# Two chained transformer blocks on one core: the modulation products in float32 on four column groups, and three of their parts moved to the input products

## The chip, the core and the metric

The kernel runs on one core of a Trainium2 chip. TensorE multiplies matrices into PSUM banks of 128 partitions by 512 float32 columns. VectorE (DVE), ScalarE (ACT) and GpSimd (POOL) work elementwise, and SyncE (SP) issues nearly all transfers from HBM to SBUF, in one order. The metric is the device time of one execution in microseconds; lower is better.

## What is computed

The reference chains two pairs of layers over 256 tokens of width 1024. In the first pair (call its layers 1 and 2) there is also a stream of 256 context tokens. Six vectors of 1024 numbers for each stream, the modulation, come from a condition vector: `m = silu(cond) @ w_mod + b_mod`, split into shift, scale and gate of the attention half and shift, scale and gate of the FFN half. They enter like this:

```python
sh1, sc1, g1, sh2, sc2, g2 = adaln(c, w_mod[l], b_mod[l])
h = modulate(rms_norm(x, norm1_g[l]), sh1, sc1)          # h * (1 + sc1) + sh1
q, k, v, up, ca, cb = project_inputs(h, w_in[l], ...)
...                                                       # differential attention, pool, conv
x = x + g1 * (mix @ w_out[l])
x = x + g2 * swiglu(modulate(rms_norm(x, norm2_g[l]), sh2, sc2), ...)
```

`w_mod[l]` is 1024 by 6144, so each of the six parts is a product of two rows (one for each stream) with a matrix of 4 MB. The second pair of layers has another attention with a table of relative biases, and a gated FFN.

## The kernel before, in words

**Arithmetic.** A float32 product is made of float32r pieces. `piece` (L192) loads 512 KB of weights into a buffer `raw` (4 buffers), ACT rounds it into the high half of a buffer `hl` (4 buffers, 8 KB a partition), and DVE subtracts to make the low half. Three products (high by high, high by low, low by high) of one pass each then stand for one float32 product. A few products are done in plain float32, which the program issues as one matmul and the engine runs as two passes.

**Order.** The kernel is written as generators that yield after each piece of work. `weave` (L1105) takes a step of a main generator and then as many steps of a side generator as a rate says. The engines' queues follow from that by a scheduler which may move instructions past each other, so the listings below are of the program as built. SP's transfers keep the written order (`dma`, L143): a transfer that waits for its buffer holds up all transfers behind it.

**Stages of layer 1.** First the start (`start`, L720): shift and scale of the attention half (2048 columns of `w_mod`) in four chunks of 2 by 256 columns (`mod`), the norm and transposes of 512 tokens (`turn`), and the input products of the convolution, two k at a time (`products`). Then the input products: queries, keys, pool and values, woven with 31 convolution taps on DVE (`conv_mix`). Then the differential attention (`diff_attention`, L1246): 16 steps (4 tiles of 128 tokens by 4 heads), each with two score products of 64 rows (upper and lower half of the array's rows), a softmax on DVE and ACT, transposes and a product with the values in bank `ob`. Woven into it, at 1.8 steps each, is `side_all`: the parts 2, 3 and 4 of the modulation (gate, and shift and scale of the FFN half) by `ada_rows_parts` (L337), 8 pieces of 2 k for each of 2 halves of 512 columns, and then the first two pieces of the output product. Then the output product and the FFN.

**The modulation's products.** In `ada_rows_parts` and `mod` the stationary operand is the condition: `cs` holds high and low parts of both streams in 4 columns. For each k, one matmul of 4 columns takes the high half of the weights and one of 2 columns the low half; both accumulate into 4 rows of a bank. `rows_to_cols` (L369) turns rows into columns by products with a selector of 4 rows (`selc`), `rows_to_gates` (L392) spreads a row over 128 partitions (`selb`).

**The relative biases.** In layer 2 the FFN's side generator `side3` runs `dil_bias` (L1376): 16 transfers of 128 KB from a table in HBM (`dbias`) to two bias tiles, with a yield after each fourth; behind it `prepare2` issues 16 small transfers of gains.

Of the kernel before, what the change touches and what calls it, by code (L numbers as in the profile page):

```python
# [9 lines left out]
F32 = mybir.dt.float32  # L10
F32R = mybir.dt.float32r
# [31 lines left out]

C_ID, C_SELC, C_COS, C_SIN, C_INVF, C_SELB, NCONST = 0, 128, 130, 258, 386, 402, 402 + 256


# [11 lines left out]
def _constants():  # L58
# [15 lines left out]
    for s in range(2):  # L74
        for r in (s, s + 2):
            k[r, C_SELC + s] = 1.0
            k[r, C_SELB + s * P:C_SELB + (s + 1) * P] = 1.0
# [19 lines left out]
class _Kernel:  # L97
    def __init__(self, ctx, tc, io, out):
        self.tc, self.nc, self.io, self.out = tc, tc.nc, io, out
        self.n = 0  # L100
        self.last = self.mark = None
        self.later, self.due = [], []
        pool = lambda name, bufs, **kw: ctx.enter_context(tc.tile_pool(name=name, bufs=bufs, **kw))
        self.big = pool("big", 12)
        self.wraw = pool("wraw", 4)
        self.whl = pool("whl", 4)
        self.s4 = pool("s4", 3)
        self.s2 = pool("s2", 6)
        self.small = pool("small", 24)
# [145 lines left out]
    def setup(self):  # L255
# [10 lines left out]
        self.invf = km[:, C_INVF:C_INVF + 16]  # L266
        self.selc = km[0:4, C_SELC:C_SELC + 2]
        self.selb = [km[0:4, C_SELB + s * P:C_SELB + (s + 1) * P] for s in range(2)]

# [6 lines left out]
        self.mhalf = self.cst.tile([P, 32], F32, tag="mhalf", name="mhalf")  # L276
        nc.gpsimd.memset(self.mhalf, -0.5)


# [8 lines left out]
        nc.vector.scalar_tensor_tensor(si, th, 1.0, cc, op0=ALU.add, op1=ALU.mult)  # L288
        self.cs = self.cst.tile([P, KD, 4], F32R, tag="cs", name="cs")
        self.csf = self.cst.tile([P, KD, 2], F32, tag="csf", name="csf")  # L290
        v = si.rearrange("p (s k) -> p k s", s=2)
        nc.vector.tensor_copy(self.csf, v)
        nc.vector.tensor_copy(self.cs[:, :, 0:2], v)
        nc.vector.tensor_sub(self.cs[:, :, 2:4], v, self.cs[:, :, 0:2].bitcast(F32))

# [25 lines left out]

    def ada_rows_native(self, l, part):
        banks = [self.bank("acc") for _ in range(2)]
        for k in range(KD):
            raw = self.load(self.wview(self.io["w_mod"][l], k, 1, part * D, (part + 1) * D), 1, D)
            for n in range(2):
                self.mm(banks[n][0:2, :], self.csf[:, k, :], raw[:, n * 512:(n + 1) * 512],
                        start=(k == 0), stop=(k == KD - 1))
            yield
        out = []  # L330
        for n in range(2):
            r = self.S2([2, 512])
            self.nc.vector.tensor_copy(r, banks[n][0:2, :])
            out.append(r)
        self._rows = (out, self.ident[0:2, 0:2])

    def ada_rows_parts(self, l, part):  # L337
        out = []
        for n in range(2):
            c0 = part * D + n * 512  # L340
            b = self.bank("acc")
            for k0 in range(0, KD, 2):
                hi, lo = self.piece(self.wview(self.io["w_mod"][l], k0, 2, c0, c0 + 512), 2, 512)
                for kk in range(2):
                    k = k0 + kk
                    self.mm(b[0:4, :], self.cs[:, k, 0:4], hi[:, kk, :], start=(k == 0), stop=False)
                    self.mm(b[0:2, :], self.cs[:, k, 0:2], lo[:, kk, :], start=False, stop=(k == KD - 1))
                yield
            r = self.S2([4, 512])
            self.nc.vector.tensor_copy(r, b[0:4, :])  # L350
            out.append(r)
        self._rows = (out, self.selc)

# [15 lines left out]
    def rows_to_cols(self, dst, bcol):  # L369

        rows, sel = self._rows
        for n in range(2):
            b = self.bank()
            for j in range(4):
                self.mm(b[:, 2 * j:2 * j + 2], rows[n][:, j * P:(j + 1) * P], sel)
# [16 lines left out]
    def rows_to_gates(self, gates):  # L392

        rows, _ = self._rows
        for n in range(2):
# [324 lines left out]
    def start(self):  # L720
# [17 lines left out]
        def mod(c):  # L738

            nonlocal cols  # L740
            rb, r = self.bank(), self.S2([4, 512])
# [10 lines left out]
            nc.scalar.copy(r[0:4, 0:256], rb[0:4, 0:256])  # L752
            if c >= 1:
                part(256, c * 256)
                nc.scalar.copy(r[0:4, 256:512], rb[0:4, 256:512])
            else:
                xload(0)
                turns = self.columns([(0, rows(io["norm1_g"][0]), 0), (KD, rows(io["b_mod"][0, 0:2 * D]), 0)], "c0_0")
                for half in range(2):
                    raw = self.load(self.wview(wm, 4 * half, 4, c * 256, (c + 1) * 256), 4, 256)  # L760
                    xload(1 + half)
                    raw = raw.rearrange("p (a b) -> p a b", a=4)
                    for kk in range(4):
                        k = 4 * half + kk
                        self.mm(rb[0:2, 256:512], self.csf[:, k, :], raw[:, kk, :], start=(k == 0), stop=(k == KD - 1))
                nc.scalar.copy(r[0:2, 256:512], rb[0:2, 256:512])
                xload(3)
                cols = turns()
                nc.vector.tensor_scalar(cols[:, 2 * KD:], cols[:, 2 * KD:], 1.0, None, op0=ALU.add)
            for j in range(2):  # L770
                k = 2 * c + j
                o = ps[:, 4 * k:4 * k + 4]
                self.mm(o[:, 0:2], r[0:4, j * P:(j + 1) * P], self.selc)
                if c >= 1:
                    self.mm(o[:, 2:4], r[0:4, 256 + j * P:256 + (j + 1) * P], self.selc)
                else:
                    nc.tensor.transpose(o[:, 2:4], r[0:2, 256 + j * P:256 + (j + 1) * P], self.ident[:2, :2])
                nc.vector.scalar_tensor_tensor(
# [171 lines left out]
    def layer1(self, l, S, xin, hT):  # L950
# [59 lines left out]
        if not last:  # L1010
            gates = [self.gate(l, 2, s) for s in streams]

            def side():
                yield from self.ada_rows_parts(l, 2)
                self.rows_to_gates(gates)
                for p, d in ((3, 2), (4, 3)):
                    yield from self.ada_rows_parts(l, p)
                    self.rows_to_cols(S.mod[:, d], S.part(p))
# [4 lines left out]
            def side_all():  # L1023
                yield from side()
                for _ in range(2):
                    next(out)
                    yield
# [76 lines left out]

    def weave(self, main, side, rate):  # L1105

        due = 0.0
        for _ in main:
            due += rate
            while due >= 1.0:  # L1110
                due -= 1.0
                next(side, None)
        for _ in side:
            pass

# [260 lines left out]
    def dil_bias(self, out):  # L1376
        a = self.dr[:, :, :]
        for qt in range(2):
# [410 lines left out]
```

## Time and profile before

| what | value |
|---|---|
| time, median of 3 runs | 1683.26 us (1681.92 to 1684.46) |
| the profiled execution | 1682.13 us, span 1680.3 us |
| TensorE busy | 1639.1 us, 98% of the span |
| DVE, ACT busy | 72%, 49% |
| transfers | 262.75 MB, mean 156 GB/s |

The span is the time between the first and last instruction. TensorE's busy time counts matmuls with modelled ends, so overlapping ones are not counted twice. "PEclk" is the granted TensorE clock: 1.00 is 2.4 GHz and 0.50 is 1.2 GHz. A stage's stretch is read with the windows view, which gives each engine's busy time in it; a single instruction's wait stands in brackets in the timeline.

### The profile page before, as it was taken

What the parts mean: (1) busy time and instruction counts of PE and PEld (TensorE: products, weight loads), DVE (VectorE), ACT (ScalarE), POOL (GpSimd) and SP (SyncE); (2) the same over time, 40 slices, a digit from 0 to 9 for tenths busy, and PEclk for the clock granted to TensorE, in tenths of its full rate; (3) what the DMA queues carried; (4) which work ended last, traced back from release to release, by engine and by line L of the source; (5) the groups of instructions that cost most, each with busy time, mean ns of one, the idle gap of its engine ahead of it and who ended that gap; (6) DMA issues with size and microseconds to landing.
All of it is one profiled execution on the core that took longest, in us unless ns stands there. A gap on an engine that the chain in (4) does not pass through costs nothing.

```text
span 1680.3 us, 24688 instructions
## 1 busy us (share of the span) xinstructions
PE 1639.1 (98%) x9399; PEld 1382.5 (82%) x9399; DVE 1205.3 (72%) x2114; ACT 830.6 (49%) x1377; POOL 41.3 (2%) x98
## 2 busy tenths in 40 slices
PE   8999999999999999999799899999999999999998
PEld 5787467878888888886698899788999988799998
DVE  6797876866585545986566557767887887578786
ACT  6344655423222223646543346765555576565553
POOL 1000000000000000000000001000000010000000
PEclk9999899999999999999899999999999999999999
DMA  8622552655375553432269755523566555245653
GB/s 265 192 86 88 184 179 63 189 170 148 124 235 176 166 175 113 139 113 75 89 219 243 199 183 163 155 88 104 188 188 189 175 149 154 70 138 187 189 180 122
DMA packets 183334, 262.75 MB, mean 156 GB/s; under 512 B 11597, under 2 KB 123184, under 8 KB 183216
## 3 DMA queue, kind: packets, MB, share of 16 engines
q1 hardware_dynamic: 182936, 260.85, 50.1%
q8 instruction: 74, 1.21, 0.3%
q10 hardware_dynamic: 280, 0.33, 0.2%
q14 instruction: 44, 0.36, 0.1%
HBM read 259.84 MB, written 1.31 MB: 155 GB/s over the span
## 4 chain that ended last, share of the span: by engine, by line
PE 80%; DVE 7%; DMA 5%; ACT 4%; issue 3%; POOL 1%; SPq 0%; ACTq 0%; DVEq 0%; POOLq 0%
PE aux L155 36%; PE acc L155 33%; PE ob L155 6%; PE aux L245 3%; DMA raw<-in_w_mod_dram 3%; DVE hl L201 2%; ACT hl L199 1%; DVE s L1208 1%; DMA raw<-in_w_ffn_in_dram 1%; DMA raw<-in_w_ffn_out_dram 1%; DMA a<-dbias 0%; ACT s L469 0%; ACT s L1268 0%; ACT jk L417 0%; DMA a<-in_x_dram 0%
## 5 line engine op out<-in xcount | busy, mean ns | idle before, releaser
L155 PE MATMUL acc<-hl,a 128*128 128x512 f32 (+3 forms) x3072 | 718.3, 386 | 7.4 <-ACT hl L199 2.4
L199 ACT CAST hl<-raw 128x1024 fp32r<-128x1024 f32 (+1 forms) x420 | 433.7, 1038 | 500.7 <-PE acc L155 151.0
L155 PEld LDWEIGHTS acc<-hl,a 128*128 128x128 f32 x3072 | 549.9, 189 | 116.6 <-issue 5.2
L201 DVE TENSOR_TENSOR hl<-raw,hl 128x1024 fp32r<-128x1024 f32 (+1 forms) x420 | 503.4, 1203 | 155.9 <-ACT hl L199 153.9
L155 PE MATMUL aux<-a,hl 128*128 128x256 f32 (+1 forms) x4032 | 578.6, 304 | 4.7 <-ACT hl L199 1.6
L155 PEld LDWEIGHTS aux<-a,hl 128*128 128x128 f32 x4032 | 540.2, 192 | 37.4 <-ACT a L470 2.0
L363 DVE SCALAR_TENSOR_TENSOR s<-raw,csf,s 128x1024 f32<-128x1024 f32 x70 | 88.7, 1281 | 43.2 <-DMA raw<-in_w_mod_dram 43.1
L245 PE MATMUL aux<-km,s 128*128 128x128 f32 (+1 forms) x416 | 66.2, 282 | 11.0 <-DVE s L451 8.0
L245 PEld LDWEIGHTS aux<-km,s 128*128 128x128 f32 (+1 forms) x416 | 48.9, 144 | 33.6 <-issue 14.9
L1208 DVE SCALAR_TENSOR_TENSOR s<-up,c,s 128x512 f32<-128x512 f32 (+1 forms) x120 | 70.8, 609 | 0.6
L155 PE MATMUL ob<-a,hl 128*128 128x512 f32 (+1 forms) x288 | 64.3, 372 | 0.0
L155 PEld LDWEIGHTS ob<-a,s 128*128 128x128 f32 x416 | 52.2, 194 | 11.2 <-ACT s L1282 5.4
L155 PEld LDWEIGHTS ob<-a,hl 128*128 128x128 f32 x288 | 51.2, 188 | 9.3
L155 PE MATMUL ob<-a,s 128*128 128x64 f32 (+1 forms) x416 | 56.2, 279 | 0.7 <-ACT s L1665 0.5
L155 PE MATMUL aux<-a,a 96*128 96x256 f32 (+2 forms) x160 | 52.5, 507 | 1.4 <-ACT s L1268 1.3
L532 ACT ACTIVATE s<-aux 128x512 f32<-128x512 f32 x33 | 19.7, 597 | 62.5 <-PE aux L155 62.5
L560 ACT ACTIVATE s<-s,c2a,c2b 128x256 f32<-128x256 f32 x88 | 48.0, 592 | 3.3 <-DVE s L557 3.3
L535 ACT CAST a<-s 128x512 fp32r<-128x512 f32 x33 | 20.4, 618 | 52.9 <-DVE s L534 52.8
L557 DVE TENSOR_TENSOR s<-aux,km 128x512 f32<-128x512 f32 x44 | 30.4, 691 | 20.9 <-PE aux L155 20.9
L533 DVE SCALAR_TENSOR_TENSOR s<-s,aux 128x512 f32<-128x512 f32 x33 | 22.6, 684 | 25.0 <-ACT s L532 25.0
L417 ACT ACTIVATE jk<-a 128x512 bf16<-128x512 f32 x44 | 28.2, 641 | 24.0 <-DVE a L1005 15.3
L1268 ACT ACTIVATE s<-aux,sm,rq 128x512 f32<-128x512 f32 (+1 forms) x48 | 33.8, 705 | 10.7 <-DVE sm L1267 10.4
(244 smaller groups left out, 1306.6 us busy)
## 6 DMA issues: line engine op xcount, KB each, us to landing
raw<-in_w_mod_dram SPq DMA_DIRECT2D x96, 512.0 KB
raw<-in_w_ffn_in_dram SPq DMA_DIRECT2D x88, 512.0 KB
raw<-in_w_up_dram SPq DMA_DIRECT2D x88, 512.0 KB
raw<-in_w_in_dram SPq DMA_DIRECT2D x60, 512.0 KB
raw<-in_w_ffn_out_dram SPq DMA_DIRECT2D x44, 512.0 KB
raw<-in_w_down_dram SPq DMA_DIRECT2D x44, 512.0 KB
raw<-in_w_out_dram SPq DMA_DIRECT2D x32, 512.0 KB
gate<-in_b_mod_dram SPq DMA_DIRECT2D x6, 512.0 KB
```

Of the source, the lines that this page charges most:

```text
L155: self.nc.tensor.matmul(o, lhsT, rhs, start=start, stop=stop)
L199: nc.scalar.copy(hl[:, 0, :n], raw[:, :n])
L201: nc.vector.tensor_sub(hl[:, 1, :n], raw[:, :n], hl[:, 0, :n].bitcast(F32))
L245: self.nc.tensor.transpose(b[:rows, j * P:(j + 1) * P], s, self.ident)
L363: self.nc.vector.scalar_tensor_tensor(accs[s], raw, c, accs[s], op0=ALU.mult, op1=ALU.add)
L417: self.nc.scalar.activation(junk, x[:, h * 512:(h + 1) * 512], AF.Square, scale=D ** -0.5, accum_out=ss[:, h:h + 1])
L533: nc.vector.scalar_tensor_tensor(th, th, 1.0, g, op0=ALU.add, op1=ALU.mult)
L535: nc.scalar.copy(hi, th)
L557: nc.vector.tensor_mul(y, x.rearrange("p (j t) -> p j t", j=2), R2)
L560: nc.scalar.activation(o[:, j, :], y[:, j, :], AF.Identity, scale=wc(1, ff), bias=bc(ff))
L1208: nc.vector.scalar_tensor_tensor(o, up[:, ct, :, k:k + SEQ], w, o, op0=ALU.mult, op1=ALU.add)
L1268: nc.scalar.activation(p[:, c, :], sb[:, :nk * P], AF.Exp, scale=r, bias=nm[:, c:c + 1], accum_out=d[:, c:c + 1])
```

## The change

In float32, without splitting: the condition is stored in `csf`, padded with zeros from 2 to 32 columns for each k. Four k's products go to the four groups of 32 partitions of one bank (`ada_products`), each as one float32 matmul, and the two products for k and k + 4 accumulate in a group. The sum over the four groups is left to the selectors, which now have ones at every 32nd row and 128 rows. The weights come unsplit: in `mod` from `raw`, in the moved parts by transfers of 1 MB into a buffer of the pool `hl`.

The parts 2, 3 and 4 move from the attention's side to a second side of the input products, at rate 1.3; the bank is `ob`. In the attention only the two pieces of the output product stay at its side. `dil_bias` yields after each second transfer. The pool of small tiles shrinks from 24 to 16 buffers.

```diff
-                for half in range(2):
-                    hi, lo = self.piece(self.wview(wm, 4 * half, 4, c0, c0 + 256), 4, 256)
-                    for kk in range(4):
-                        k = 4 * half + kk
-                        self.mm(rb[0:4, o:o + 256], self.cs[:, k, 0:4], hi[:, kk, :], start=(k == 0), stop=False)
-                        self.mm(rb[0:2, o:o + 256], self.cs[:, k, 0:2], lo[:, kk, :], start=False, stop=(k == KD - 1))
+                for half in range(2):
+                    raw = self.load(self.wview(wm, 4 * half, 4, c0, c0 + 256), 4, 256)
+                    self.ada_products(rb[:, o:o + 256], 4 * half, raw.rearrange("p (a b) -> p a b", a=4))
...
+    def ada_products(self, o, k0, raw):
+        for j in range(4):
+            k = k0 + j
+            self.mm(o[j * GROUP:(j + 1) * GROUP, :], self.csf[:, k, :], raw[:, j, :], start=(k < 4), stop=(k >= 4))
+
+    def ada_rows(self, l, part):
         out = []
         for n in range(2):
             c0 = part * D + n * 512
-            b = self.bank("acc")
-            for k0 in range(0, KD, 2):
-                hi, lo = self.piece(self.wview(self.io["w_mod"][l], k0, 2, c0, c0 + 512), 2, 512)
...
+            b = self.bank("ob")
+            for k0 in range(0, KD, 4):
+                raw = self.whl.tile([P, 2, 1024], F32, tag="hl", name=self.nm("wm_"))
+                raw = raw.rearrange("p a (b c) -> p (a b) c", c=512)
+                self.dma(raw, self.wview(self.io["w_mod"][l], k0, 4, c0, c0 + 512))
+                self.ada_products(b, k0, raw)
+                yield
...
-        self.weave(main(), self.conv_mix(S, TQ, len(streams), mB), TAPS[l])
+        self.weave(main(), self.conv_mix(S, TQ, len(streams), mB), TAPS[l], () if last else mods(), 1.3)
...
-            self.weave(self.diff_attention(S, qT, kT, v, rq, q_toks, mA, LAG), side_all(), 1.8)
+            self.weave(
+                self.diff_attention(S, qT, kT, v, rq, q_toks, mA, LAG), (next(out) for _ in range(2)), 0.25)
...
-                if q % (4 * COPIES) == 3 * COPIES:
+                if q // COPIES % 2:
                     yield
```

How the order moves is seen at three places. On TensorE, between the first two pieces of the queries (`hl` is a split piece of `w_in`, `acc` the four banks of the projection, `a` the normalised input), before:

```order
L155 MATMUL acc_735<-hl_738,a_12_149 128x512 x2
L155 MATMUL acc_735<-hl_738,a_14_151 128x512
L155 MATMUL acc_732<-hl_772,a_12_149 128x512 x2
L155 MATMUL acc_732<-hl_772,a_14_151 128x512
L155 MATMUL acc_733<-hl_772,a_12_149 128x512 x2
L155 MATMUL acc_733<-hl_772,a_14_151 128x512
```

and in the changed kernel (`wm` is a piece of `w_mod` as it was loaded):

```order
L156 MATMUL acc_639<-hl_642,a_12_147 128x512 x2
L156 MATMUL acc_639<-hl_642,a_14_149 128x512
L156 MATMUL ob_674<-wm_675,csf 32x512 x4
L156 MATMUL acc_636<-hl_683,a_12_147 128x512
L156 MATMUL acc_637<-hl_683,a_12_147 128x512
```

A group of four products, one on each column group, has come between two pieces of the projection; there are 12 such groups in this stage. On TensorE at the beginning of the attention (`aux<-a,a` is a score product, `cs` the condition), before:

```order
L155 MATMUL aux_1518<-a_114_728,a_113_727 128x512
L155 MATMUL aux_1523<-a_114_728,a_113_727 128x512
L155 MATMUL acc_1531<-hl_1534,cs 4x512
L155 MATMUL acc_1531<-hl_1534,cs 2x512
L155 MATMUL aux_1545<-a_114_728,a_113_727 128x512
L155 MATMUL acc_1531<-hl_1560,cs 4x512
L155 MATMUL acc_1531<-hl_1560,cs 2x512
```

and in the changed kernel (`hl_1637` is a piece of `w_out`):

```order
L156 MATMUL aux_1544<-a_100_628,a_99_627 128x512
L156 MATMUL aux_1549<-a_100_628,a_99_627 128x512
L156 MATMUL aux_1561<-a_100_628,a_99_627 128x512
L156 MATMUL acc_1631<-hl_1637,a_96_622 128x512 x2
L156 MATMUL acc_1631<-hl_1637,a_97_623 128x512
L156 MATMUL acc_1632<-hl_1637,a_96_622 128x512
L156 MATMUL aux_1566<-a_100_628,a_99_627 128x512
L156 MATMUL aux_1578<-a_100_628,a_99_627 128x512
```

The 96 products with `cs` are gone from between the scores, and products of the first pieces of `w_out` stand there earlier. Of the 16 pairs of score products, 10 stood side by side before; now 7 do. On SP in layer 2's FFN (`dbias` the bias table, `raw` weights of the FFN), before:

```order
L147 DMA a_1258_7707<-dbias 16x8x256 x4
L147 DMA raw_7718<-in_w_ffn_out_dram 128x2x512
L147 DMA raw_7735<-in_w_ffn_out_dram 128x2x512
L147 DMA a_1258_7707<-dbias 16x8x256 x4
L147 DMA raw_7759<-in_w_ffn_in_dram 128x4x256
L147 DMA raw_7788<-in_w_ffn_in_dram 128x4x256
```

and in the changed kernel:

```order
L148 DMA a_1208_7463<-dbias 16x8x256 x2
L148 DMA raw_7472<-in_w_ffn_out_dram 128x2x512
L148 DMA raw_7489<-in_w_ffn_out_dram 128x2x512
L148 DMA a_1208_7463<-dbias 16x8x256 x2
L148 DMA raw_7511<-in_w_ffn_in_dram 128x4x256
L148 DMA raw_7540<-in_w_ffn_in_dram 128x4x256
```

Two bias transfers instead of four go between two weight transfers, so that 16 weight transfers are spread among them where 8 were.

## Rows read from the trace of the kernel before

**Rows 1.** The page, part 1: busy time, share and instructions of each engine.

```profile
PE 1639.1 (98%) x9399; PEld 1382.5 (82%) x9399; DVE 1205.3 (72%) x2114; ACT 830.6 (49%) x1377; POOL 41.3 (2%) x98
```

**Rows 2.** Windows by stage: us; PE, PEld, DVE, ACT, POOL; clock, DMA share, GB/s.

```profile
0.00:35.00 35.00, 26.83 (x160) 17.78 (x160) 21.51 (x44) 21.61 (x39) 4.79 (x21) 0.90 0.80 265
35.00:68.00 33.00, 31.79 (x162) 23.66 (x162) 23.20 (x55) 14.34 (x21) 0.20 (x1) 1.00 0.70 222
68.00:162.70 94.70, 94.33 (x482) 79.15 (x481) 83.53 (x145) 40.46 (x64) 2.62 (x5) 1.00 0.34 105
162.70:260.40 97.70, 94.10 (x431) 52.27 (x430) 78.78 (x177) 63.25 (x120) 3.60 (x6) 0.95 0.50 167
191.75:202.00 10.25, 10.25 (x25) 4.61 (x24) 6.59 (x12) 3.19 (x4) 0.00 (x0) 0.50 0.19 55
762.20:803.20 41.00, 40.16 (x192) 25.24 (x192) 29.09 (x76) 24.53 (x51) 2.66 (x6) 1.00 0.25 77
```

**Rows 3.** Windows, instructions on `cs` alone (PE, PEld, DVE), in the attention.

```profile
162.70:260.40 97.70, 27.12 (x96) 7.50 (x96) 0.00 (x0) 0.95 0.50 167
```

**Rows 4.** Timeline of TensorE in the attention: start, us, instruction, [idle before].

```profile
163.73 1.13 PE L155 MATMUL aux<-a,a 64*128 64x512 f32 x4
164.79 1.08 PE L155 MATMUL acc<-hl,cs 128*4 128x512 f32 x4
165.80 1.12 PE L155 MATMUL aux<-a,a 64*128 64x512 f32 x2
166.85 1.33 PE L155 MATMUL acc<-hl,cs 128*4 128x512 f32 x5
...
172.30 2.01 PE L155 MATMUL acc<-hl,cs 128*2 128x512 f32 x8
174.28 1.12 PE L155 MATMUL aux<-a,a 64*128 64x512 f32 x2
176.49 1.09 PE L155 MATMUL acc<-hl,cs 128*4 128x512 f32 x4 [1.09 <-ACT hl L199]
```

**Rows 5.** Groups by shape, attention (162.7 to 260.4 us): busy us, mean ns.

```profile
L155 PE MATMUL aux<-s,km 4*128 4x512 f32 x8 | 5.8, 855 | 0.0
L155 PE MATMUL aux<-km,s 4*128 4x2 f32 x32 | 4.2, 249 | 0.0
...
L201 DVE TENSOR_TENSOR hl<-raw,hl 128x1024 fp32r<-128x1024 f32 x27 | 32.3, 1213 | 0.6 <-ACT hl L199 0.5
```

**Rows 6.** Groups by shape, the half-clock stretch, 191.75 to 202.00 us.

```profile
L155 PE MATMUL aux<-s,km 4*128 4x512 f32 x4 | 3.8, 1096 | 0.0
L155 PE MATMUL aux<-a,a 64*128 64x512 f32 x4 | 2.1, 1138 | 0.0
```

**Rows 7.** Groups by shape, whole span: plain float32 products of 128 rows.

```profile
L155 PE MATMUL aux<-s,ones 128*128 128x512 f32 x16 | 7.5, 592 | 0.0
...
L155 PE MATMUL aux<-raw,csf 128*2 128x256 f32 x16 | 3.8, 379 | 0.0
```

**Rows 8.** Timeline of TensorE in the start.

```profile
47.59 2.00 PE L155 MATMUL aux<-hl,cs 128*4 128x256 f32 x16
```

**Rows 9.** Windows of layer 2's FFN around the bias transfers.

```profile
920.00:935.00 15.00, 12.03 (x76) 10.30 (x74) 7.78 (x9) 5.30 (x6) 0.00 (x0) 1.00 1.12 220
935.00:950.00 15.00, 12.10 (x59) 10.63 (x60) 7.93 (x23) 4.60 (x5) 0.00 (x0) 0.77 0.53 157
935.86:939.27 3.41, 3.41 (x18) 3.41 (x18) 0.30 (x1) 0.00 (x0) 0.00 (x0) 0.50 0.13 42
946.10:949.50 3.40, 3.40 (x9) 2.65 (x9) 3.40 (x19) 2.09 (x2) 0.00 (x0) 0.50 0.89 281
```

**Rows 10.** The chain of waits, 895 to 965 us: start, us, what.

```profile
912.84 13.54 DMA raw<-in_w_ffn_in_dram
...
928.80 9.65 DMA raw<-in_w_ffn_out_dram
```

More of the change, by code (lines that the diff above doesn't have):

```diff
@@ L44 @@
 C_ID, C_SELC, C_COS, C_SIN, C_INVF, C_SELB, NCONST = 0, 128, 130, 258, 386, 402, 402 + 256
+GROUP = 32
 def _bucket(rel):
@@ L74, in _constants @@
     for s in range(2):
-        for r in (s, s + 2):
+        for r in range(s, P, GROUP):
             k[r, C_SELC + s] = 1.0
@@ L108, in __init__ @@
         self.s2 = pool("s2", 6)
-        self.small = pool("small", 24)
+        self.small = pool("small", 16)
         self.cst = pool("cst", 1)
@@ L266, in setup @@
         self.invf = km[:, C_INVF:C_INVF + 16]
-        self.selc = km[0:4, C_SELC:C_SELC + 2]
-        self.selb = [km[0:4, C_SELB + s * P:C_SELB + (s + 1) * P] for s in range(2)]
+        self.selc = km[:, C_SELC:C_SELC + 2]
+        self.selb = [km[:, C_SELB + s * P:C_SELB + (s + 1) * P] for s in range(2)]
         self.R = km[:, C_SELB:C_SELB + SEQ]
@@ L320, in ada_bias @@
         self.dma(dst, self.io["b_mod"][l:l + 1, part * D:(part + 1) * D].partition_broadcast(P))
[L322 to L337, printed above, removed]
+    def ada_products(self, o, k0, raw):
[3 more added lines that the diff above has]
+    def ada_rows(self, l, part):
         out = []
@@ L340, in ada_rows_parts @@
             c0 = part * D + n * 512
-            b = self.bank("acc")
-            for k0 in range(0, KD, 2):
-                hi, lo = self.piece(self.wview(self.io["w_mod"][l], k0, 2, c0, c0 + 512), 2, 512)
[L344 to L347, printed above, removed]
+            b = self.bank("ob")
[4 more added lines that the diff above has]
+                self.ada_products(b, k0, raw)
                 yield
-            r = self.S2([4, 512])
-            self.nc.vector.tensor_copy(r, b[0:4, :])
+            r = self.S2([P, 512])
+            self.nc.vector.tensor_copy(r, b)
             out.append(r)
-        self._rows = (out, self.selc)
+        self._rows = out
     def ada_sums(self, l, part, streams):
@@ L369, in rows_to_cols @@
     def rows_to_cols(self, dst, bcol):
-        rows, sel = self._rows
+        rows = self._rows
         for n in range(2):
@@ L392, in rows_to_gates @@
     def rows_to_gates(self, gates):
-        rows, _ = self._rows
+        rows = self._rows
         for n in range(2):
@@ L740, in mod @@
             nonlocal cols
-            rb, r = self.bank(), self.S2([4, 512])
+            rb, r = self.bank(), self.S2([P, 512])
             def part(o, c0):
                 for half in range(2):
-                    hi, lo = self.piece(self.wview(wm, 4 * half, 4, c0, c0 + 256), 4, 256)
-                    for kk in range(4):
-                        k = 4 * half + kk
-                        self.mm(rb[0:4, o:o + 256], self.cs[:, k, 0:4], hi[:, kk, :], start=(k == 0), stop=False)
-                        self.mm(rb[0:2, o:o + 256], self.cs[:, k, 0:2], lo[:, kk, :], start=False, stop=(k == KD - 1))
-            part(0, D + c * 256)
[L752 to L756, printed above, removed]
+                    raw = self.load(self.wview(wm, 4 * half, 4, c0, c0 + 256), 4, 256)
+                    self.ada_products(rb[:, o:o + 256], 4 * half, raw.rearrange("p (a b) -> p a b", a=4))
+            part(0, D + c * 256)
+            nc.scalar.copy(r[:, 0:256], rb[:, 0:256])
+            if c == 0:
                 xload(0)
                 turns = self.columns([(0, rows(io["norm1_g"][0]), 0), (KD, rows(io["b_mod"][0, 0:2 * D]), 0)], "c0_0")
-                for half in range(2):
[L760 to L767, printed above, removed]
+            part(256, c * 256)
+            nc.scalar.copy(r[:, 256:512], rb[:, 256:512])
+            if c == 0:
+                for t in range(1, 4):
+                    xload(t)
                 cols = turns()
@@ L772, in mod @@
                 o = ps[:, 4 * k:4 * k + 4]
[L773 to L777, printed above, removed]
+                self.mm(o[:, 0:2], r[:, j * P:(j + 1) * P], self.selc)
+                self.mm(o[:, 2:4], r[:, 256 + j * P:256 + (j + 1) * P], self.selc)
                 nc.vector.scalar_tensor_tensor(
@@ L988, in layer1, with mods @@
         v = []
-        self.weave(main(), self.conv_mix(S, TQ, len(streams), mB), TAPS[l])
+        if not last:
+            gates = [self.gate(l, 2, s) for s in streams]
+        def mods():
+            yield from self.ada_rows(l, 2)
+            yield
+            self.rows_to_gates(gates)
+            for p, d in ((3, 2), (4, 3)):
+                yield from self.ada_rows(l, p)
+                yield
+                self.rows_to_cols(S.mod[:, d], S.part(p))
+        self.weave(main(), self.conv_mix(S, TQ, len(streams), mB), TAPS[l], () if last else mods(), 1.3)
         self.flush()
@@ L1103, in reload, with weave @@
         return r
-    def weave(self, main, side, rate):
-        due = 0.0
+    def weave(self, main, *sides):
+        sides = [[iter(s), rate, 0.0] for s, rate in zip(sides[::2], sides[1::2])]
         for _ in main:
[L1109 to L1114, printed above, removed]
+            for x in sides:
+                x[2] += x[1]
+                while x[2] >= 1.0:
+                    x[2] -= 1.0
+                    next(x[0], None)
+        for x in sides:
+            for _ in x[0]:
+                pass
     def pool_mix(self, S, stat, w_in, q_toks, band, mB, ready, ahead):
```

24 lines of the change are left out of this document (5 added, 19 removed).

## The prediction, made before the changed kernel ran

> **What bounds the kernel now.** I read the page's busy shares first, then the windows of the stages that the change touches, then the timeline of TensorE, the groups by shape and the chain of waits where an engine waits. TensorE is busy for 98% of the span [rows 1], so a change counts for what it does to TensorE's queue: matmul time, waits and half clock. In the input products (68 to 162.7 us) it waits for 0.4 us, while DVE has 83.5 of 94.7 us of work [rows 2]. In the attention (162.7 to 260.4 us) it waits for 97.7 - 94.1 = 3.6 us, and the mean clock is 0.95 [rows 2]: from 191.75 to 202.00 us it is 0.50, that is 1.2 GHz instead of 2.4, and all of that stretch is busy [rows 2]. One of the waits is at 176.49 us, 1.09 us before products on `cs`, ended by ACT's rounding of their weights [rows 4]: the modulation's own split is late there. The start is bound differently: in its first 35 us TensorE has 26.8 us of work and the transfers run at 265 GB/s [rows 2]. A last place is in layer 2's FFN, 920 to 950 us: TensorE is idle for 2.97 and 2.90 us, and for two times 3.4 us at half clock [rows 9]; the chain of waits goes through two weight transfers of 13.54 and 9.65 us, issued between the bias transfers [rows 10].
>
> **The change part by part.** All sums are against the profiled execution's 1682.13 us, which is 1.1 us under the median of the three runs.
>
> *Attention, removed.* The 96 products on `cs` have 27.12 us of busy time [rows 3], but the modelled ends overlap what follows; eight in a row take 172.30 to 174.28, 0.248 us each [rows 4], which for 96 makes 23.8. Some ran at half clock, so I take 25.5, between the two. Their waits: of the 3.6 us idle I take 2.7, since nothing else in the stage needs a split of `w_mod`. The half clock of other work: the stretch's 10.25 us, less 3.8 of gates [rows 6] and some 2.4 on `cs`, leave 4 us of scores, value products and transposes, which at full clock take 2; 2 us are saved. That assumes that the clock does not fall again. The 8 passes that spread the gates cost 5.8 us [rows 5], 3.8 of them for four at half clock [rows 6]; at full clock all 8 take 4.0. They move, so the attention loses 5.8 and the input products gain 4.0; the 32 passes that turn rows into columns (4.2 us [rows 5]) move at the same price. DVE loses 24 of its 27 subtractions of 1.213 us [rows 5], ACT as many roundings: 29 us of DVE which stay off the sum, because it isn't the bound there.
>
> *Attention, added.* A pair of score products side by side, one on the upper and one on the lower 64 rows, takes 1.06 us (163.73 to 164.79), and a single one 1.05 (165.80 to 166.85) [rows 4]: two at once for the price of one. The new order has three pairs fewer side by side. One is of 512 columns and two are of 256, of half the size: about 1 + 1.3 us. Then the filler is gone. What remains for TensorE is 94.1 - 25.5 - 5.8 - 4.2 - 2 + 2.3 = 59 us for 16 steps, for DVE at most 78.8 - 29 = 50 us [rows 2, 5], so TensorE should stay the bound. The nearest row is the attention of layer 2, which has only `w_out` as filler: idle 0.84 of 41 us at clock 1.00 [rows 2]. Against it, steps of 256 keys with nothing between them come here. I take 3 us of new waits; the bounds are 0.5 (that row, scaled) and 15 (waits and a fall of the clock).
>
> *Input products, added.* 12 groups of four float32 products of 512 columns. The trace before has no product on column groups, so the price is bounded by rows. One plain float32 product of 512 columns on a part of the array's rows takes 1.05 us, two passes of 0.53; two on different rows at once 1.06 [rows 4]. If four column groups run at once like those, a group takes 1.06 plus three short loads, 1.2 us; 12 make 14.4. If they run one after the other, a group takes 8 passes of 0.47 (16 in 7.5 us [rows 7]) to 0.53, that is 3.8 to 4.2 us, and 12 make 45 to 51. I take 1.2, by the pair of rows, which is the only case of two small products at once in this trace. With the gates' 4.0 and 2 us of waits for weights (a group's megabyte waits for one of four buffers of `hl`, and SP holds the next piece of `w_in` behind it; the lead is one to two pieces of 5.7 us, 24 products at 0.24) the stage grows by 20.4, and by the 4.2 that only change place. DVE's 83.5 us plus ten copies and additions of about 0.7 fit in 119.
>
> The Trainium skill, "TensorE: Matmul & The Clock Gate", Part 3, speaks on both sides of this. Its measured speedups give 2.38 for three column tiles; with the same yield for four (2.38 / 3 x 4 = 3.2) a group would be an estimated 1.06 x 4 / 3.2 = 1.3 us, and the stage 1 us longer than I have it. Its list of what overlaps says that a weight load overlaps running products only where the row group differs. Column groups share all rows, so by that rule the loads, and then the products, would stand in line; that is the first rival below. The pair in [rows 4] differs in rows and bears out neither against the other.
>
> *Start.* 112 products on `cs` of 256 columns (16 in 2.00 us [rows 8]: 14.0 us) and 16 passes of 3.8 us [rows 7] become 16 groups of 256 columns at about 0.63: 10 us. Only what lies behind 35 us counts, where TensorE is the bound (31.8 of 33 us [rows 2]): 32 products or 4.0 us become four groups or 2.5. Before that, chunk 1 waits for the transposes as now, and the splits that ACT and DVE made between them go. Against it, a `raw` buffer now comes free only when TensorE has used it, so the second piece of `w_in` is issued behind the last chunk's first product and TensorE may wait some 2 us for it. I take -2, between -5 and +4.
>
> *Bias transfers.* In 920 to 950 us 5.9 us are idle and 6.8 us run at half clock [rows 9], worth 3.4: 9.3 us in all. With twice as many weight transfers between them, the same 2 MB of bias cost half as much of the weights' rate at any time; the queue of 16 small transfers behind them stays. I take 5 of the 9.3, between 0 and 9.
>
> *Nothing, with cover:* the selectors of 128 rows have as many columns and passes as those of 4; the smaller pool of small tiles only adds waits between instructions that TensorE's queue covers.
>
> Sum: start -2; attention -25.5 - 5.8 - 2.7 - 2 + 2.3 + 3 = -30.7; input products +20.4; bias -5. Together -17.3, or 1664.8 us for the profiled execution. I predict 1665 us.
>
> **The rivals.** *One after the other (slower).* The column groups do not run at once. The place is the 12 groups between pieces of `w_in`, where TensorE has no slack (0.4 us idle), and the chunks of the start. 12 groups at 3.8 to 4.2 instead of 1.2 us add 31 to 36 us; the start's 16 groups at 8 x 0.24 = 1.9 us add 8 on the path. That is 1704 to 1709, say 1707 us. It decides as soon as a group takes more than about 2.6 us. For it: nothing in this trace shows column groups at work. Against it: half arrays do run at once. *Two at a time.* The array takes the four streams in two turns: 12 x 2.1 = 25 instead of 14.4, and some of the start: 1677 us. *The attention starves.* Without the products on `cs` TensorE waits on the softmax and the clock falls: 15 us of the 30.7 are lost, 1677 to 1680. For it: scores now stand close together, with three banks `aux` for scores and transposes. Against it: layer 2's attention [rows 2].
>
> **How the numbers follow.** The forecast has 0.64, one after the other 0.14, two at a time 0.11, the starved attention 0.08, and 0.03 for a gain over 35 us. The forecast's own range is 1652 to 1676: the bounds of the start, of the bias and of the waits, taken together. The range 1648 to 1688 takes in the two middle cases and leaves out the slow rival. A measurement of this kernel tells about 0.2%, 3.4 us, from no change. Faster by more: 0.79; within: 0.07; slower: 0.14.
>
> **What would show it.** A group of four on `wm` takes about 1.2 us from its first start to the next matmul, with starts a few ns apart; eight starts 0.5 us apart would prove the slow rival. The input products grow from 95 to about 119 us, and TensorE stays busy in them. The attention from first score to last value product shrinks from 97 to about 63 us without half clock. In the FFN of layer 2 idle time falls to 2 or 3 us. The prediction is wrong if a group takes over 2 us, or if waits in the attention exceed 8 us.

## The result and the profile after

| kernel | median | runs | against the kernel before |
|---|---|---|---|
| before | 1683.09 us | 1681.92 to 1684.46 | |
| changed | 1700.89 us | 1700.17 to 1703.42 | 1.0108, 95% interval 1.0091 to 1.0126 |

The change makes the kernel 17.8 us slower, where 18 us faster were forecast. All medians in this document are of fast runs; one run of a later kernel (new_start_alone), of 3215 us, is left out as slow. The page's part 1 of the changed kernel answers to [rows 1]; DVE and ACT lost the work that the splits were, and TensorE gained nothing:

```profile
PE 1641.2 (96%) x9401; PEld 1382.7 (81%) x9401; DVE 1164.6 (68%) x2074; ACT 794.3 (47%) x1339; POOL 40.9 (2%) x99
```

Where the time went is found by matching each matmul of one trace with the same matmul of the other. The changed trace is 7.6 us behind at the first input product, 7.0 to 7.6 us from 280 to 920 us of the trace before, and 21.6 us from 979 us on, to the end. So time is lost in two places, the start and layer 2's FFN, and the pair of stages that was to bring the gain, input products and attention, wins nothing. The windows by stage of the changed kernel, with the columns of [rows 2]: the start to 35 us, its rest, the input products, layer 1's attention, and the FFN of layer 2 around the bias transfers:

```profile
0.00:35.00 35.00, 25.32 (x162) 17.75 (x162) 12.89 (x37) 12.89 (x30) 5.16 (x22) 0.75 0.68 228
35.00:75.87 40.87, 34.24 (x170) 24.33 (x162) 16.45 (x48) 10.32 (x17) 0.20 (x1) 0.84 0.66 221
75.87:193.06 117.19, 117.04 (x621) 86.54 (x621) 90.26 (x162) 41.26 (x64) 1.72 (x5) 1.00 0.58 202
193.06:268.14 75.08, 67.45 (x298) 42.00 (x298) 47.41 (x135) 39.46 (x95) 3.61 (x6) 0.93 0.09 29
912.12:1006.55 94.43, 80.77 (x486) 72.27 (x485) 42.40 (x62) 29.30 (x34) 0.20 (x1) 0.89 0.64 172
```

The same work of that FFN in the kernel before took 80.00 us, in the same view:

```profile
905.00:985.00 80.00, 74.13 (x487) 67.54 (x486) 42.16 (x61) 30.46 (x34) 0.21 (x1) 0.96 0.79 201
```

The reader is to see three things. The clock of the start is 0.75 and 0.84, where it was 0.90 and 1.00 [rows 2], and the stage ends later. The input products grew from 95.4 to 117.2 us with TensorE always busy, about as forecast, but the attention shrank from 96.6 (first score to last value product) to 75.1 only, with 75.08 - 67.45 = 7.6 us of idle time and a clock of 0.93. And the FFN has 94.43 - 80.77 = 13.7 us of idle time instead of 5.9, and 20.5 us at half clock instead of 6.8, which costs another 6.8; these two make up its 14.4 us.

**The groups of four.** Timeline of TensorE in the input products, and the group by shape over the whole span:

```profile
81.95 1.06 PE L156 MATMUL ob<-wm,csf 128*32 128x512 f32 x8
82.95 1.81 PE L156 MATMUL acc<-hl,a 128*128 128x512 f32 x6
...
L156 PE MATMUL ob<-wm,csf 128*32 128x512 f32 x96 | 13.6, 603 | 0.0
```

Four products in two passes each (x8) take 82.95 - 81.95 = 1.00 us, with the four starts of a pass 7 ns apart. The column groups run at once; the slow rival is not what made the kernel slow. That its 1707 us is near the measured time is chance.

**The attention.** Timeline of TensorE in its second half; waits in brackets, ended by ACT's exponentials (L1245):

```profile
239.50 0.70 PE L156 MATMUL aux<-a,a 64*128 64x256 f32 x2
240.12 0.49 PE L156 MATMUL acc<-hl,a 128*128 128x512 f32 x1
242.24 0.93 PE L156 MATMUL aux<-a,a 64*128 64x256 f32 x2 [1.62 <-ACT s L1245]
243.09 2.93 PE L156 MATMUL acc<-hl,a 128*128 128x512 f32 x6
...
260.07 1.22 PE L156 MATMUL aux<-a,a 64*128 64x256 f32 x2 [2.04 <-ACT s L1245]
```

With only pieces of `w_out` left as filler, score products wait for a bank that a softmax still reads (4.5 of the 7.6 us), and around the two longest of these waits the clock falls: 243.09 shows six products in 2.7 us to the next start, where six take 1.5 at full clock (219.70 to 221.16 us). Half clock holds for 3.4 us there and for 6.83 us from 259.63, within the second wait.

**The FFN of layer 2.** Timelines of the changed kernel, TensorE and then ACT. L200 rounds weights, L522 is the gate's tanh, L525 rounds the result:

```profile
941.23 7.28 PE L156 MATMUL aux<-a,hl 128*128 128x256 f32 x46 [0.76 <-DVE hl L202]
950.89 0.73 PE L156 MATMUL acc<-hl,a 128*128 128x512 f32 x2 [2.38 <-ACT hl L200]
...
949.27 0.62 ACT L525 CAST a<-s 128x512 fp32r<-128x512 f32 x1 [8.40 <-DVE s L524]
949.80 3.88 ACT L200 CAST hl<-raw 128x1024 fp32r<-128x1024 f32 x4
964.84 0.60 ACT L522 ACTIVATE s<-aux 128x512 f32<-128x512 f32 x1 [11.16 <-PE aux L156]
965.33 1.98 ACT L200 CAST hl<-raw 128x1024 fp32r<-128x1024 f32 x2
974.21 0.62 ACT L525 CAST a<-s 128x512 fp32r<-128x512 f32 x1 [6.89 <-DVE s L524]
```

ACT takes its queue in order: it is idle for 11.16 us before the tanh at 964.84 us, and the two roundings behind it follow at once. Between L525 and the next L522 stand four roundings, and two behind it: the weights of the next products are rounded only when the tanh has had its gate products, so TensorE runs dry each time. In the regular stretches of this FFN it is three and three, one rounding ahead of need. With the bias on SP's queue, ACT's queue has one such irregular place with the old yield and three with the new one, in every trace kept; the start, the parts and the pool of small tiles leave it as it is. The loaded weights lie ready: the four roundings at 949.80 follow each other without a wait. After 956.8 us no bias transfer is issued any more, and the waits of 2.4 us at 950.89 and 975.83 are alike.

### The profile page after: what moved, and what is told of

Read it like the earlier page. It is cut to its first block, busy times and chain, and to the rows that moved or that the text cites. A ratio compares the mean times of both kernels' runs of the same rounds, so it can differ in the third digit from the quotient of the medians.

```text
span 1701.6 us, 24528 instructions
## 1 busy us (share of the span) xinstructions
PE 1641.2 (96%) x9401; PEld 1382.7 (81%) x9401; DVE 1164.6 (68%) x2074; ACT 794.3 (47%) x1339; POOL 40.9 (2%) x99
## 4 chain that ended last, share of the span: by engine, by line
PE 80%; DVE 7%; issue 7%; ACT 3%; DMA 2%; POOL 1%; ACTq 0%; POOLq 0%; DVEq 0%
PE aux L156 38%; PE acc L156 32%; PE ob L156 7%; PE aux L246 3%; DVE hl L202 2%; DVE s L1185 1%; DMA raw<-in_w_mod_dram 1%; ACT hl L200 1%; ACT s L459 1%; DVE s L353 0%; POOL sm L163 0%; ACT jk L407 0%; DMA raw<-in_w_ffn_out_dram 0%; ACT s L1245 0%; POOL sm L420 0%
## 5 line engine op out<-in xcount | busy, mean ns | idle before, releaser
L156 PE MATMUL acc<-hl,a 128*128 128x512 f32 (+3 forms) x3072 | 727.9, 388 | 12.1 <-ACT hl L200 6.4
L200 ACT CAST hl<-raw 128x1024 fp32r<-128x1024 f32 (+2 forms) x382 | 393.3, 1037 | 454.9 <-PE aux L156 143.5
L202 DVE TENSOR_TENSOR hl<-raw,hl 128x1024 fp32r<-128x1024 f32 (+2 forms) x382 | 457.1, 1203 | 154.9 <-ACT hl L200 153.1
L522 ACT ACTIVATE s<-aux 128x512 f32<-128x512 f32 x33 | 19.7, 597 | 83.2 <-PE aux L156 83.2
L525 ACT CAST a<-s 128x512 fp32r<-128x512 f32 x33 | 20.4, 619 | 58.9 <-DVE s L524 58.8
L1245 ACT ACTIVATE s<-aux,sm,rq 128x512 f32<-128x512 f32 (+1 forms) x48 | 33.8, 707 | 23.0 <-DVE sm L1244 22.7
L156 PE MATMUL acc<-a,hl 128*128 128x512 f32 (+1 forms) x192 | 39.2, 362 | 1.9 <-ACT hl L200 1.0
```

Of the source, the lines that this page charges most:

```text
L156: self.nc.tensor.matmul(o, lhsT, rhs, start=start, stop=stop)
L200: nc.scalar.copy(hl[:, 0, :n], raw[:, :n])
L202: nc.vector.tensor_sub(hl[:, 1, :n], raw[:, :n], hl[:, 0, :n].bitcast(F32))
L522: nc.scalar.activation(th, g, AF.Tanh, scale=0.5)
L525: nc.scalar.copy(hi, th)
L1245: nc.scalar.activation(p[:, c, :], sb[:, :nk * P], AF.Exp, scale=r, bias=nm[:, c:c + 1], accum_out=d[:, c:c + 1])
```

## The experiments

Each ran beside the kernel before; ratios are to it, with 95% intervals. "Stages" are from the profiled executions.

**1. The yield, taken back.** In the changed kernel:

```diff
-                if q // COPIES % 2:
+                if q % (4 * COPIES) == 3 * COPIES:
```

> The changed kernel with the yield of the bias transfers as before (after each fourth). Theory A: this yield alone changes the order of ACT's queue in layer 2's FFN (the gate's tanh comes ahead of the rounding of the next weights), and that is the 14.4 us by which the two traces drift apart between 905 and 985 us; then this kernel takes 1686 to 1688 us, and its trace stays 7 us behind that of the kernel before, from the attention of layer 1 to the end. Theory B: the FFN of layer 2 loses its time for another reason (it starts later, with other buffers); then 1699 to 1702 us.

1689.44 us, 1.0039 (1.0027 to 1.0051): 11.5 us less than the changed kernel. The trace ends 7.1 us behind. That is theory A, 1.4 us above its range.

**2. The new yield alone,** in the kernel before, the same two lines the other way round:

> The kernel before with nothing but the new yield of the bias transfers (after each second). Theory A: 14 us are lost in layer 2's FFN here too, 1696 to 1698 us. Theory B: 1683 us. By the term of my forecast: 1678 us.

1695.55 us, 1.0081 (1.0055 to 1.0107): 12.3 us more than the 1683.22 beside it. The waits of the stretch 900 to 1000 us, in us, times and longest, are those of the changed kernel (4.9, 4.8, 3.0 and 1.1 there):

```profile
PE aux L155 <- ACT hl L199: 4.9, 3, 1.6
PE acc L155 <- ACT hl L199: 4.8, 2, 2.4
PE aux L155 <- DVE hl L201: 3.0, 3, 1.5
PE acc L155 <- DVE hl L201: 0.7, 2, 0.5
```

Theory A holds (0.5 us under its range), and my term of -5 us has the wrong sign. The yield is shown to be the cause; that it acts through ACT's order is read from the traces, and no run changes that order alone.

**3. The bias from another queue,** in the kernel of 1 and in the kernel before:

```diff
-                self.dma(t[q:q + COPIES], src)
+                self.nc.gpsimd.dma_start(t[q:q + COPIES], src)
```

> The changed kernel with the yield as before, and the 16 bias transfers issued from GpSimd's queue instead of SP's. In the order of ACT's queue the tanh of every gate then has three roundings of weights ahead of it and three behind, as in the rest of this FFN. Theory A: then layer 2's FFN loses neither the 5.9 us of idle time nor the 6.8 us at half clock that the kernel before has there: 9 us less than with the yield as before alone, 1679 to 1681 us. Rival (it is the 2 MB of bias on the transfer engines that make the weights late, whatever queue issues them): 1688 to 1690 us.

> The kernel before with nothing changed but the 16 bias transfers, which GpSimd's queue issues instead of SP's. Theory A: the 9.3 us of waits and half clock of the FFN of layer 2 go here too: 1673 to 1675 us. Rival: the gain of 9 us with the changed kernel came from its own order: 1682 to 1684 us.

1680.35 us, 0.9988 (0.9978 to 0.9999), 9.1 us less than experiment 1; and 1673.91 us, 0.9943 (0.9923 to 0.9962), 9.2 us less than the kernel before: theory A both times. The window of the same work of the FFN in the first of the two takes 69.69 us instead of 80.00 and 94.43, with nothing idle; then the 16 issues (duration in ns, first and last start):

```profile
915.38:985.07 69.69, 69.69 (x487) 64.88 (x487) 43.33 (x62) 30.50 (x34) 0.21 (x1) 1.00 0.66 204
...
L1362 POOL DMA_DIRECT2D a<-dbias x16: 530/530/758, 831.7 to 845.5; - x16
```

GpSimd issues the 16 transfers from 831.7 to 845.5 us, some 70 us earlier than SP did (903.0 to 927.4 in the kernel before), since no weight transfer stands ahead of them. ACT's queue has no irregular place any more. Two things change together here, the order on ACT and the time of the transfers; they weren't separated.

**4. The start as before,** with the parts moved and the old yield (weights through `piece`, products on `cs`):

> The three parts in float32 on column groups and moved to the input products; the start (weights split by ACT and DVE, products on the condition's high and low parts) and the yield of the bias transfers are those of the kernel before. By the terms of my forecast (-30.7 + 20.4) 10 us faster than the kernel before, 1673 us. Theory S and F together (the new start costs 7 us; the attention without its filler waits 7.6 us and runs 10 us at half clock, so that the move gives next to nothing): 1681 to 1684 us. Rival: the new start costs nothing that the old one would not cost here: 1688 to 1690 us, as with the new start.

1691.63 us, 1.0058 (1.0041 to 1.0076): neither theory; the rival comes nearest, and the old start is even 2.2 us slower here than the new one in experiment 1. Its start has the same order on TensorE as that of the kernel before, and yet it has 13.7 us of half clock instead of 6.8, the input products begin at 75.51 us, and they take 121.29 instead of 117.19 us. Two more runs, start_before and moved_alone, were to have the old start as well; their edit left the new one in place, so they only repeat, with two small instructions more on DVE, the changed kernel (1702.52 us) and experiment 1 (1690.05 us).

**5. Buffers or clock at the start.** Two edits to the kernel of 1; first the weights in buffers of `hl`, then filler:

```diff
+                raw = self.whl.tile([P, 2, 1024], F32, tag="hl", name=self.nm("wm_"))
                 for half in range(2):
-                    raw = self.load(self.wview(wm, 4 * half, 4, c0, c0 + 256), 4, 256)
...
                 x = res[t // 2][:, t % 2, :]
+                self.warm(10)
```

> The changed kernel with the yield as before, and the start's weights of the modulation loaded into buffers of hl (8 KB a partition, both halves of a part in one) instead of raw, so that 4 MB of weights can be under way ahead of TensorE instead of 2 MB. Theory buffers (the start is late because a raw buffer is held until TensorE has used it: from 20 to 30 us the transfers run at 21 GB/s): 5 to 7 us less than with the yield as before alone, 1682 to 1684 us. Theory clock (the start is late because TensorE has too little to do and runs at half clock for 30 us): 1688 to 1690 us.

> The changed kernel with the yield as before, and 40 products of ones (128 columns) that nothing reads, ten ahead of the transposes of each of the start's four tiles, so that TensorE is not idle there. Theory clock: the clock stays at 1.00 through the transposes and chunk 1, which save 4 to 6 us: 1683 to 1686 us. Theory buffers: the clock may stay up, but the first input products still wait for their weights: 1688 to 1690 us.

1688.97 us (1.0026, 1.0011 to 1.0041) and 1688.55 us (1.0039, 1.0026 to 1.0051): both medians are within 1 us of experiment 1, more buffers in the range of theory clock and filler in that of theory buffers, so neither theory holds alone. The rest of the start in experiment 1, then the start with more buffers, then with filler:

```profile
35.00:75.54 40.54, 33.83 (x163) 24.42 (x163) 16.45 (x48) 10.32 (x17) 0.20 (x1) 0.84 0.67 225
```

```profile
0.00:35.00 35.00, 24.48 (x164) 16.83 (x164) 13.75 (x38) 13.45 (x31) 5.13 (x22) 0.77 0.86 288
35.00:71.59 36.59, 31.84 (x162) 23.14 (x161) 15.62 (x47) 9.81 (x16) 0.20 (x1) 0.89 0.59 205
```

```profile
0.00:35.00 35.00, 30.63 (x256) 23.92 (x260) 13.84 (x38) 13.46 (x31) 5.25 (x22) 0.93 0.76 256
35.00:74.83 39.83, 34.27 (x152) 25.44 (x144) 15.53 (x46) 10.01 (x15) 0.20 (x1) 0.80 0.61 209
```

More buffers bring more bytes early (288 GB/s instead of 228) and 4 us in the profiled start (75.54 to 71.59), of which the median keeps 0.5. The median hides two groups: four of the ten runs, the profiled one (1686.47 us) among them, took 1684.2 to 1686.5 us, the others 1688.8 to 1691.4. What decides between them stays open. Filler lifts the clock of the first 35 us to 0.93; then it falls behind them, and 0.7 us are left, so this run did not hold the clock up and does not clear it.

**6. The new start alone,** in the kernel before_bias_gpsimd (pool of 16 small tiles; parts split and in the attention):

> The kernel of before_bias_gpsimd with the new start (16 groups of products on column groups, weights unsplit in raw, pool of 16 small tiles); the three parts stay split and in the attention. Theory S (with the new start TensorE runs at half clock for 30 us instead of 7, and the input products begin 6 us later): 5 to 7 us more than before_bias_gpsimd, 1679 to 1681 us. By my forecast: 2 us less. Rival (the old start falls to half clock just as well in other executions, as in before_new_yield and moved_only): within 2 us of before_bias_gpsimd.

1679.34 us, 0.9975 (0.9963 to 0.9987): 5.4 us more, as theory S has it; but the pool of small tiles changes with the start here. Windows of this start, and then of the old one beside it:

```profile
0.00:35.00 35.00, 24.92 (x162) 16.57 (x162) 12.72 (x39) 12.57 (x30) 5.13 (x22) 0.71 0.70 234
35.00:74.41 39.41, 34.26 (x166) 24.82 (x162) 16.97 (x47) 11.22 (x18) 0.20 (x1) 0.83 0.63 210
```

```profile
0.00:35.00 35.00, 28.59 (x156) 18.73 (x156) 19.91 (x40) 20.40 (x37) 4.79 (x21) 0.85 0.75 246
35.00:70.48 35.48, 32.83 (x169) 24.09 (x168) 24.74 (x59) 15.75 (x22) 0.20 (x1) 1.00 0.69 227
```

**7. Parts back in the attention,** on column groups, in the kernel bias_on_gpsimd_queue; first parts 3 and 4 (at rate 0.7), then all three, as shown:

```diff
+            def fill():
+                yield from self.ada_rows(l, 2, "acc")
+                yield
+                self.rows_to_gates(gates)
+                ...
+                for _ in range(2):
+                    next(out)
+                    yield
+            self.weave(self.diff_attention(S, qT, kT, v, rq, q_toks, mA, LAG), fill(), 1.0)
```

> The kernel of bias_on_gpsimd_queue with parts 3 and 4 (8 of the 12 groups) back in the attention, on column groups in banks acc, at a rate of 0.7 a step, ahead of the first two pieces of the output product. Theory F (the attention starves without filler: 7.6 us idle, 10.2 us at half clock): the input products get 10 to 11 us shorter, and the attention takes the 8 groups for nearly nothing: 8 to 11 us less than bias_on_gpsimd_queue, 1669 to 1672 us. Rival (the waits belong to the softmax's own chain and stand elsewhere than the filler): 1678 to 1681 us.

> As two_parts_in_attention, with all three parts (12 groups and the gates) in the attention at a rate of 1.0, none in the input products: the float32 products on column groups where the split ones were. Theory F: the idle time of the attention is used up by then, so the last four groups and the gates cost as much there as in the input products: within 2 us of two_parts_in_attention, 1668 to 1674 us. Rival: the order with the gates' passes among the scores costs more: 1675 us and above.

1673.28 us, 0.9940 (0.9919 to 0.9961), and 1666.08 us, 0.9901 (0.9880 to 0.9922): 7.1 and 14.3 us less than with all parts moved. Windows of the input products and of the attention with all parts moved, then with three parts in the attention:

```profile
77.86:195.07 117.21, 117.05 (x620) 86.52 (x621) 90.26 (x162) 41.14 (x64) 1.72 (x5) 1.00 0.57 197
195.07:270.46 75.39, 67.78 (x299) 42.53 (x299) 47.40 (x135) 39.46 (x95) 3.61 (x6) 0.93 0.09 29
```

```profile
74.84:170.16 95.32, 94.94 (x485) 79.70 (x485) 80.69 (x142) 38.48 (x61) 1.73 (x5) 1.00 0.31 97
170.16:254.23 84.07, 82.72 (x428) 45.54 (x428) 55.93 (x155) 41.54 (x97) 3.60 (x6) 1.00 0.58 201
```

In the attention the three parts, gates included, cost 84.07 - 75.39 = 8.7 us over the stage without them; in the input products 117.21 - 95.32 = 21.9. Idle time is 1.35 us instead of 7.6 and the clock 1.00. That is theory F, but for one point: it had the last four groups gain nothing more, and they gain as much as the first eight (7.2 after 7.1 us).

**8. One column group.** The kernel bias_on_gpsimd_queue with all products of the moved parts on the first group:

```diff
-                self.ada_products(b, k0, raw)
+                for j in range(4):
+                    k = k0 + j
+                    self.mm(b[0:GROUP, :], self.csf[:, k, :], raw[:, j, :], start=(k == 0), stop=(k == KD - 1))
```

> The kernel of bias_on_gpsimd_queue with the 96 float32 products of the moved parts all on the first column group, eight in a row into 32 rows of the bank; only these rows are copied and used. If four groups really run side by side (starts 7 ns apart in the trace of the changed kernel), four such products now take 8 passes of 0.47 to 0.53 us, 3.8 to 4.2 instead of 1.05 us; 12 groups add 33 to 38 us: 1713 to 1718 us, and the input products take 150 to 155 us. If the groups run one after the other and the trace only shows their starts early: 1680 us.

1711.70 us, 1.0173 (1.0144 to 1.0203). Timeline of TensorE:

```profile
80.70 3.62 PE L156 MATMUL ob<-wm,csf 128*32 128x512 f32 x8
84.25 5.73 PE L156 MATMUL acc<-hl,a 128*128 128x512 f32 x24
```

The same eight passes take 3.55 us instead of 1.00; over 12 groups that is 30.6 us, and the kernel took 31.4 more.

**9. Together.** The kernel of three_parts_in_attention with the old start, and with the new one in more buffers:

> The kernel of three_parts_in_attention with the start of the kernel before (split weights). Theory S (the new start costs 5.4 us, new_start_alone against before_bias_gpsimd): 1660 to 1662 us. Rival (the clock falls in the start at other times in other programs, whichever start they have): 1664 to 1668 us.

> The kernel of three_parts_in_attention with the new start, its weights in buffers of hl as in start_more_buffers. If the new start is late by its buffers: 1661 to 1663 us. If it is late by TensorE's clock alone: 1665 to 1667 us.

1666.22 us, 0.9900 (0.9875 to 0.9926), the rival's range; and 1663.34 us, 0.9886 (0.9866 to 0.9906), next to the range of the buffers. The second beats both kernels, by 19.0 us the kernel before that ran beside it. The old start is no better than the new one here: its input products begin at 73.31 instead of 74.84 us, but take 99.44 instead of 95.32. Its timeline shows why, the first two rows of the stage:

```profile
73.31 1.20 PE L158 MATMUL acc<-hl,a 128*128 128x512 f32 x4 [1.62 <-ACT hl L202]
76.35 4.21 PE L158 MATMUL acc<-hl,a 128*128 128x512 f32 x9 [1.84 <-DVE hl L204]
```

Two split pieces of `w_in` come late, and then nine products take 4.2 us at half clock, which holds for 6.8 us, from 75.1 us on.

## Why the prediction was wrong

Medians of pairs that differ in one step give a ledger; for "parts moved" the two kernels ran in different sessions:

| step | forecast | measured | from |
|---|---|---|---|
| new start | -2 | +5.4 | new_start_alone less before_bias_gpsimd |
| products on column groups, in their old place | (not apart) | -13.3 | three_parts_in_attention less new_start_alone |
| parts moved | (not apart) | +14.3 | bias_on_gpsimd_queue less three_parts_in_attention |
| the two together | -10.3 | +1.0 | |
| yield of the bias transfers | -5 | +11.5 to +12.3 | experiments 1 and 2 |
| sum | -17.3 | +17.9 to +18.7 | the change itself: +17.8 |

The split between the first three rows depends on the order of the steps. With the old start, products and move together cost 8.8 us (experiment 4 against the kernel before), and the new start then gains 2.2 (experiment 1 against experiment 4). Either way the three rows lose 6.4 to 6.6 us together, where -12.3 were forecast.

**Bias transfers (17 us off).** This step failed most: "with twice as many weight transfers between them, the same 2 MB of bias cost half as much of the weights' rate". I took two long weight transfers in the chain of waits [rows 10] for the cause of the idle time in [rows 9]. The waits end mostly with ACT's rounding, which in the changed kernel is of weights that have landed; the yields set how ACT's queue is ordered, and more yields made two more badly ordered places: +11.5 to +12.3 us. I read only SP's order of this stage.

**Attention (12 us off).** "TensorE should stay the bound", with 3 us of new waits, was the failed step; 7.6 us of waits came, and 10.2 us at half clock, which cost some 5 more, together near the upper bound of 15 that I had given. The mean busy times of TensorE (59 us) and DVE (50 us) said nothing on the chain score, softmax, transpose of each step. Layer 2's attention, on which I leaned, has 0.84 us of idle time with a filler of `w_out` throughout. The rival of the starved attention was right in kind, and I gave it 0.08.

**Input products (right).** 117.2 us against 119. The group took 1.00 us instead of 1.2. By the Trainium skill, "TensorE: Matmul & The Clock Gate", Part 3, a weight load overlaps running products only where the row group differs. The trace decides against that: in the first group the loads of the second pass start from 81.98 us on, while the first pass, on the same 128 rows, runs from 81.95 to 82.57 us. From the rule I had argued that the four products would stand in line; they start 7 ns apart, and experiment 8 shows what standing in line costs. The wait for the stage's first weights, for which the start's term allowed 2 us, is 1.6.

**Start (7 us off by one pair, its size not settled).** Forecast between -5 and +4, measured +5.4 by one pair, about 0 and -2.2 by two others (experiments 9 and 4). I had noted that a `raw` buffer is held until TensorE has used it, but priced only one wait. In the changed kernel the transfers run at 21 GB/s from 20 to 30 us (147 in the kernel before), and the lighter products leave TensorE idle ahead of the transposes, which then run at half clock from 14 us on, for 30.7 us in all up to the input products (6.8 in the kernel before). More buffers help by 0.5 us in one pair and 2.7 in another (experiments 5 and 9); warming alone by 0.9. In the kernels with the new parts the old start wins nothing (experiments 4 and 9): its input products begin late too, and take 4 us longer. What splits the 5.4 us into clock and buffers, and why the last product of the old start ends anywhere from 68.3 to 73.9 us with the same order on TensorE, stays open. One rival was never run by itself, the pool of small tiles, which I had put at nothing: every kernel with the new start or the moved parts has 16, and the two late old starts (experiments 4 and 9) have 16 as well, while the three early ones have 24.

**Rivals.** One after the other: false (a group takes 1.00 us; experiment 8). Two at a time: false. The attention starves: true, but it was one of three causes. What I missed is that two more steps could each lose what the products gained. Neither of the two signs of being wrong that I had named came up (1.00 us a group, 7.6 us of waits in the attention): they looked at neither the start nor the FFN, nor at half clock.

## What to carry to other kernels

Filler is worth what the stage around it would otherwise wait: the same 12 groups cost 8.7 us where TensorE waits on a softmax and 21.9 where it is already full, so work that is made cheaper should stay in the stage with the gaps. A yield that spaces out transfers on SP also moved the roundings on ACT here: where a stage waits for roundings of weights, read the order of the rounding engine against the step that it stands behind, not only that of the transfers. Transfers that wait for nothing are worth trying on a queue in which nothing waits ahead of them: here that gave 9 us, with ACT's order mended by the same edit.

## What the runs showed of the hardware

Four float32 products of 32 columns on four column groups, all with the same 128 rows, run at once: 1.00 us for four, 3.55 on one group. The granted clock of the start varies between executions and programs with the same order on TensorE: half clock (1.2 of 2.4 GHz) for 6.8 us in the kernel before and for 10.2 us in before_new_yield and in before_bias_gpsimd, with input products beginning at 68.28, 70.84 and 70.48 us. It also falls around short waits: in the attention without its filler the longest waits are 1.62 and 2.04 us, and half clock follows or sets in within them, for 10.2 us in all; with the 12 groups back, 1.35 us are idle and none is at half clock. And 16 transfers of 128 KB on GpSimd's queue were issued at 0.53 us each and took 8.4 us (median) to land; TensorE waits for nothing in the FFN window of experiment 3.
